# Three of eight granules of a down projection chunk by seven block products

## The chip, the cores and the metric

The kernel runs on one core of a Trainium2 chip. Its metric is the time of one execution on the device, in microseconds (us); smaller is better. The engines are named as the profile names them: PE (matmuls; PEld is its weight load), DVE, ACT, POOL, and SP, whose queue issues most transfers.

## The reference

One encoder layer for 256 tokens of 2048 channels in float32. A mixing sub-layer (gated short convolution and grouped attention side by side, gates, one merging projection) is followed by a squared-ReLU MLP:

```
h = rmsnorm(x, norm_mlp_pre[l])
f = jnp.square(jax.nn.relu(h @ w_up[l])) @ w_down[l]
x = x + rmsnorm(f, norm_mlp_post[l])
```

`w_up` is 2048 x 8192 and `w_down` 8192 x 2048. The change is in `f`, in the product with `w_down`.

## The kernel before

**Precision.** Each float32 operand is split into two float32r parts: hi is the value rounded (a copy on ACT), lo is the rest (a subtraction on DVE; `split`, lines 73 to 82). A product is then three matmuls: hi by hi, hi by lo, lo by hi.

**Granules and chunks.** Weights come in pieces of 128 x 512 per k-tile. A granule is two k-tiles: one transfer of 512 KB into a buffer `raw` (4 of them), one ACT copy into `whi`, one DVE subtraction into `wlo`, each 128 x 1024 (`weights`, line 137). A chunk is 512 output columns over 16 k-tiles, that is 8 granules. `granule` (line 121) hands out the `whi`/`wlo` buffers: from one ring of 4 in the mixing stage, and from two rings of 4 (`wts` and `wts2`, taken in turns of 4 granules) from the gates on.

**Two forms of a chunk.** `linear` (line 154) keeps tokens on the partitions of the result: for each granule 2 token halves x 2 k-tiles x 3 matmuls of 512 columns, lines 166 to 168. `linear_channels` (line 182) keeps channels there: 4 x 2 x 3 matmuls of 256 columns, lines 196 to 203. The last merging chunk, the first up chunk and the last down chunk use a `lag` of 4 granules: the second token half runs 4 granules behind the first.

**Order.** Code is written in program order, and a list scheduler sets each engine's order and the waits; on the chip DVE and ACT run theirs in that order. The MLP runs for q = 0 to 3: 4 up chunks (the first of all by `hidden`, the others by `hidden_channels`) that write the squared ReLU `f`, split, into the pair `A`, then 4 down chunks (`down`, line 666). At a down chunk's end `done` copies (q = 0, line 673) or adds (line 675) each token half into `facc`; for q = 3 it also takes squares on ACT and multiplies by a gain (line 680 or 683), and after the last chunk `finish` (line 655) scales and stores.

**Handover.** Between the merging projection and the MLP, `residual` (line 588) makes the MLP's normalised input `x2T` (pair `C`) for each token half: sum of squares, a power on POOL, 4 scaled additions (line 593), transposes on PE (line 598), a multiplication by a gain (line 601) and a split. The first up chunk's first token half needs that of t = 0, its second half that of t = 1.

Of the kernel before, what the change touches and what calls it, by code (L numbers as in the profile page):

```python
# [32 lines left out]
def trunk_kernel(  # L33
# [25 lines left out]
    WARM = 9  # L59

# [40 lines left out]
    step_in = [False]  # L101
# [19 lines left out]
    def granule():  # L121

        n = count[0]
        count[0] += 1
        pool = rings[n // WB % len(rings)]
        if pool is wts:
            return [pool.tile([P, KG, CH], F32R, name=name) for name in ("whi", "wlo")]
        if n % WB:
            return [pool.tile([P, KG, CH], F32R, name=name, bufs=WB - 1) for name in ("whi", "wlo")]
        out = []  # L130
        for name, spare, at in (("whi0", 32, (16, 32)), ("wlo0", 48, (48, 0))):
            flat = pool.tile([P, KG * CH + spare], F32R, tag=name, name=name[:3], bufs=1)
            at = at[step_in[0]]
            out.append(flat[:, at : at + KG * CH].rearrange("p (k c) -> p k c", k=KG))
        return out

    def weights(wv, k0, k1, ahead=None):

        for kd in range(k0, k1, KD):
# [6 lines left out]
            for kg in range(0, KD, KG):  # L146
                hi, lo = granule()
# [34 lines left out]
    def linear_channels(act, wv, done):  # L182
# [25 lines left out]
        end = []  # L208
        for gran in weights(wv, 0, KT):
# [6 lines left out]
        for c in range(0, CH // P, 2):  # L216
# [4 lines left out]
            tick(END // 2)  # L221

# [386 lines left out]
    rstd2_row = late.tile([P, T], F32, name="rstd2_row")  # L609
# [9 lines left out]
    facc = big.tile([P, 2, NT, D], F32, tag="B", name="facc")[:, 0]  # L619
# [3 lines left out]
    def hidden_channels(q, j, fT):  # L623


        def done(c, acc):
# [5 lines left out]
            split(f, fT[0][:, d : d + 2, :], fT[1][:, d : d + 2, :])  # L632

# [32 lines left out]
    def down(q, j, fT):  # L666
# [98 lines left out]
```

## Time and profile before

| what | value |
|---|---|
| median of 3 runs | 1597.08 us (1595.76 to 1598.09) |
| the profiled execution, its own time | 1597.23 us |
| its span, first to last instruction | 1595.5 us |
| PE busy | 1579.0 us (99%) |
| DVE busy | 947.7 us (59%) |
| ACT busy | 710.2 us (45%) |
| mean granted clock of PE | 0.998 of full speed |

Busy times are of the span. What PE shows as busy includes matmuls that overlap each other, so the pace of matmuls is read from their starts.

### The profile page before, as it was taken

What the parts mean: (1) busy time and instruction counts of PE and PEld (TensorE: products, weight loads), DVE (VectorE), ACT (ScalarE), POOL (GpSimd) and SP (SyncE); (2) the same over time, 40 slices, a digit from 0 to 9 for tenths busy, and PEclk for the clock granted to TensorE, in tenths of its full rate; (3) what the DMA queues carried; (4) which work ended last, traced back from release to release, by engine and by line L of the source; (5) the groups of instructions that cost most, each with busy time, mean ns of one, the idle gap of its engine ahead of it and who ended that gap; (6) DMA issues with size and microseconds to landing.
All of it is one profiled execution on the core that took longest, in us unless ns stands there. A gap on an engine that the chain in (4) does not pass through costs nothing.

```text
span 1595.5 us, 26862 instructions
## 1 busy us (share of the span) xinstructions
PE 1579.0 (99%) x11210; PEld 1468.5 (92%) x11210; DVE 947.7 (59%) x1107; ACT 710.2 (45%) x860; POOL 35.7 (2%) x23
## 2 busy tenths in 40 slices
PE   9999999999999999999999999999999999999997
PEld 7899999999999999999987799889988998899986
DVE  6767676677765554555554865446654565555654
ACT  7444444545454444444443644444433444334441
POOL 0110101001000000000000000000000000000000
PEclk9999999999999999999999999999999999999999
DMA  8655545555576565666763656656566665556662
GB/s 316 210 178 166 186 151 188 176 183 187 159 250 192 193 195 189 197 197 192 253 208 104 221 194 199 197 188 193 188 196 196 189 196 191 193 186 199 196 201 84
DMA packets 86297, 306.28 MB, mean 192 GB/s; under 512 B 9632, under 2 KB 10016, under 8 KB 85920
## 3 DMA queue, kind: packets, MB, share of 16 engines
q1 hardware_dynamic: 84608, 300.32, 58.1%
q10 hardware_dynamic: 1568, 4.25, 0.8%
q8 instruction: 87, 1.43, 0.4%
q14 instruction: 34, 0.28, 0.0%
HBM read 302.44 MB, written 2.10 MB: 191 GB/s over the span
## 4 chain that ended last, share of the span: by engine, by line
PE 97%; DVE 1%; DMA 1%; POOL 0%; ACT 0%; issue 0%; SPq 0%; DVEq 0%; POOLq 0%; ACTq 0%
PE acc L200 20%; PE acc L203 20%; PE acc L196 20%; PE acc L167 12%; PE acc L168 12%; PE acc L166 12%; DMA raw<-in_w_up 1%; PE at L402 0%; PE at L400 0%; PE at L401 0%; PE tr L433 0%; DMA raw<-in_w_in 0%; PE tr L245 0%; DVE wlo L77 0%; POOL rs L257 0%; ACT whi L76 0%
## 5 line engine op out<-in xcount | busy, mean ns | idle before, releaser
L77 DVE TENSOR_TENSOR wlo<-raw,whi 128x1024 fp32r<-128x1024 f32 (+1 forms) x561 | 684.4, 1222 | 563.1 <-ACT whi L76 562.3
L76 ACT CAST whi<-raw 128x1024 fp32r<-128x1024 f32 (+1 forms) x561 | 588.4, 1050 | 738.2 <-PE acc L200 366.8
L196 PE MATMUL acc<-A,whi 128*128 128x256 f32 x1280 | 355.9, 278 | 0.0
L203 PE MATMUL acc<-A,wlo 128*128 128x256 f32 x1280 | 353.8, 276 | 0.0
L200 PE MATMUL acc<-A,whi 128*128 128x256 f32 x1280 | 353.8, 276 | 0.0
L196 PE MATMUL acc<-C,whi 128*128 128x256 f32 x1216 | 336.8, 277 | 0.0
L203 PE MATMUL acc<-C,wlo 128*128 128x256 f32 x1216 | 336.6, 277 | 0.0
L200 PE MATMUL acc<-C,whi 128*128 128x256 f32 x1216 | 336.6, 277 | 0.0
L166 PE MATMUL acc<-whi,A 128*128 128x512 f32 x704 | 274.2, 391 | 2.2 <-ACT whi L76 2.2
L167 PE MATMUL acc<-wlo,A 128*128 128x512 f32 x704 | 275.2, 391 | 1.0 <-DVE wlo L77 1.0
L168 PE MATMUL acc<-whi,A 128*128 128x512 f32 x704 | 275.0, 391 | 0.0
L196 PEld LDWEIGHTS acc<-A,whi 128*128 128x128 f32 x1280 | 240.6, 188 | 0.2
L200 PEld LDWEIGHTS acc<-A,whi 128*128 128x128 f32 x1280 | 240.4, 188 | 0.2
L203 PEld LDWEIGHTS acc<-A,wlo 128*128 128x128 f32 x1280 | 240.3, 188 | 0.0
L196 PEld LDWEIGHTS acc<-C,whi 128*128 128x128 f32 x1216 | 228.7, 188 | 0.2
L200 PEld LDWEIGHTS acc<-C,whi 128*128 128x128 f32 x1216 | 228.7, 188 | 0.2
L203 PEld LDWEIGHTS acc<-C,wlo 128*128 128x128 f32 x1216 | 228.7, 188 | 0.0
L167 PEld LDWEIGHTS acc<-wlo,A 128*128 128x128 f32 x704 | 132.2, 188 | 30.9 <-DVE wlo L77 2.8
L166 PEld LDWEIGHTS acc<-whi,A 128*128 128x128 f32 x704 | 131.9, 188 | 30.8 <-ACT whi L76 3.1
L168 PEld LDWEIGHTS acc<-whi,A 128*128 128x128 f32 x704 | 132.2, 188 | 27.8
L196 PE MATMUL acc<-B,whi 128*128 128x256 f32 x256 | 70.7, 276 | 0.0
L200 PE MATMUL acc<-B,whi 128*128 128x256 f32 x256 | 70.7, 276 | 0.0
(144 smaller groups left out, 1115.6 us busy)
## 6 DMA issues: line engine op xcount, KB each, us to landing
raw<-in_w_in SPq DMA_DIRECT2D x207, 512.0 KB, 4.3
raw<-in_w_up SPq DMA_DIRECT2D x128, 512.0 KB, 3.5
raw<-in_w_dn SPq DMA_DIRECT2D x128, 512.0 KB, 3.3
raw<-in_w_oc SPq DMA_DIRECT2D x32, 512.0 KB, 4.5
raw<-in_w_oa SPq DMA_DIRECT2D x32, 512.0 KB, 4.2
raw<-in_w_mg SPq DMA_DIRECT2D x32, 512.0 KB, 4.4
xj<-in_x SPq DMA_DIRECT2D x4, 512.0 KB, 9.6
xr<-in_x ACTq DMA_DIRECT2D x1, 2048.0 KB, 9.7
```

The source lines that it names most:

```text
L76: nc.scalar.copy(hi, src)
L77: nc.vector.tensor_tensor(lo, src, hi.bitcast(F32), op=ALU.subtract)
L166: nc.tensor.matmul(accs[t], lhsT=ah[:, a, ts_], rhs=wh[:, g, :], start=first, stop=False)
L167: nc.tensor.matmul(accs[t], lhsT=ah[:, a, ts_], rhs=wl[:, g, :], start=False, stop=False)
L168: nc.tensor.matmul(accs[t], lhsT=al[:, a, ts_], rhs=wh[:, g, :], start=False, stop=last)
L196: nc.tensor.matmul(acc, lhsT=wh[:, g, cs], rhs=ah[:, a, :], start=a == 0 and c % 2 == 0, stop=False, skip_group_check=True,)
L200: nc.tensor.matmul(acc, lhsT=wh[:, g, cs], rhs=al[:, a, :], start=False, stop=False, skip_group_check=True)
L203: nc.tensor.matmul(acc, lhsT=wl[:, g, cs], rhs=ah[:, a, :], start=False, stop=a == KT - 1, skip_group_check=True)
```

## The change

In 15 of the 16 down chunks (not the last of q = 3) the granules of k-tiles 4, 8 and 12 are multiplied as 2 x 2 blocks: two token halves by two k-tiles, two k-tiles by two halves of 256 columns. In place of 8 block products of 256 columns (24 matmuls, issued as 12 of 512 columns) there are seven (21 matmuls of 256 columns), between sums of blocks:

- `seven` makes four sums of weight blocks on DVE (128 x 256 each) and splits 7 blocks in place of 4. Its buffers, `shi`, `slo` and `u`, are two each.
- `token_sums` makes four sums of token blocks of `f` in the up chunks (128 x 128 each) and splits them, 3 times for each q.
- `linear_sevens` adds the products into four banks of PSUM: the chunk's two accumulators and two more (`x1`, `x2`). `share` and the new lines of `done` add these into `facc` at the chunk's end.

The buffers change with it. The second ring `wts2` is closed before the MLP, whose granules then take one ring of 4, and whose up chunks take their first granule from `shi`/`slo`. The first up chunk so takes its first granules from `wts` and not from `wts2`. The pair `B` becomes two tiles.

```diff
+    def seven(raw):
+        hi, lo = [sevens[0].tile([P, 7, HC], F32R, name=name) for name in ("shi", "slo")]
+        u = sevens[0].tile([P, 4, HC], F32, name="u")
+        b = raw.rearrange("p k (n c) -> p (k n) c", n=2)
+        nc.vector.tensor_tensor(u[:, 0, :], b[:, 0, :], b[:, 1, :], op=ALU.add)
+        nc.vector.tensor_tensor(u[:, 2, :], b[:, 1, :], b[:, 3, :], op=ALU.add)
+        nc.vector.tensor_tensor(u[:, 1, :], u[:, 0, :], b[:, 3, :], op=ALU.add)
+        nc.vector.tensor_tensor(u[:, 3, :], u[:, 1, :], b[:, 2, :], op=ALU.add)
+        split(b[:, 0, :], hi[:, 0, :], lo[:, 0, :])
+        split(b[:, 2:4, :], hi[:, 1:3, :], lo[:, 1:3, :])
+        split(u, hi[:, 3:7, :], lo[:, 3:7, :])
+        return hi, lo
...
+            if a in BY_SEVEN:
+                w = [(hi[:, i, :], lo[:, i, :]) for i in range(7)]
+                r = [(x[0], x[1]) for x in (sums(BY_SEVEN.index(a), i) for i in range(4))]
+                last = a == BY_SEVEN[-1]
+                mm(x1[:, 0, :], tile_of(a, 0), w[0], 2, last)
+                mm(own[0], tile_of(a + 1, 0), w[1], 0, False)
+                mm(own[1], r[3], w[2], 0, False)
+                mm(x1[:, 1, :], r[0], w[3], 2, last)
+                mm(x2[:, 0, :], r[1], w[4], 3, last)
+                mm(x2[:, 1, :], r[2], w[5], 3, last)
+                mm(own[2], tile_of(a + 1, 1), w[6], 1, False)
...
+    merging.close()
+    rings.pop()
+    mlp = ctx.enter_context(tc.tile_pool(name="mlp", bufs=2))
...
+        r = wk.tile([P, 4, P], F32, tag="cc", bufs=CCB, name="cc")
+        nc.vector.tensor_tensor(r[:, 0, :], a21, a22, op=ALU.subtract)
+        nc.vector.tensor_tensor(r[:, 1, :], a11, r[:, 0, :], op=ALU.subtract)
+        nc.vector.tensor_tensor(r[:, 2, :], a21, a11, op=ALU.subtract)
+        nc.vector.tensor_tensor(r[:, 3, :], a12, r[:, 1, :], op=ALU.subtract)
+        split(r, rsum[:, n, 0], rsum[:, n, 1])
...
+            nc.scalar.copy(e[:, 0, :], x1[:, 0, :])
+            nc.vector.tensor_tensor(w[:, 0, :], x2[:, 0, :], e[:, 0, :], op=ALU.subtract)
+            nc.vector.tensor_tensor(e[:, 1, :], x1[:, 1, :], w[:, 0, :], op=ALU.add)
+            nc.vector.tensor_tensor(w[:, 0, :], x2[:, 1, :], w[:, 0, :], op=ALU.add)
+            nc.vector.tensor_tensor(w[:, 1, :], x1[:, 1, :], w[:, 0, :], op=ALU.add)
...
+                if t == 0:
+                    nc.vector.tensor_tensor(fj, fj, shared[0].rearrange("p n c -> p (n c)"), op=ALU.add)
+                else:
+                    nc.vector.tensor_tensor(f0, f0, shared[1][:, 0, :], op=ALU.subtract)
+                    nc.vector.tensor_tensor(f1, f1, shared[1][:, 1, :], op=ALU.add)
...
-    step_in[0] = True
-    rings.reverse()
+        if q == 3 and j == 3:
+            linear(fT, w_dn[j], done, q * KT, (q + 1) * KT, lag=LAG)
+        else:
+            linear_sevens(fT, sums, w_dn[j], done, q * KT)
```

Three places show how the order moves. Line numbers differ between the two kernels: 77 is 79 after the change, 582 is 660, 593 is 671, 601 is 679, 675 is 792, and 166 to 168 are 192 to 194.

First, DVE's order at the handover, from the residual of t = 0 to that of t = 1. Before (`acc_9348` is the last merging chunk's second token half, and `wlo_9597` to `wlo_9633` are the first four granules of the first up chunk):

```order
L593 SCALAR_TENSOR_TENSOR mg_9024<-mg_9024,rows1_8878,xr_8879 128x512
L77 TENSOR_TENSOR C_8881<-cc_9497,C_8881 128x4x128
L77 TENSOR_TENSOR wlo_9597<-raw_9594,whi_9596 128x1024
L601 TENSOR_TENSOR cc_9507<-at_9502,ch_104 128x512
L77 TENSOR_TENSOR wlo_9609<-raw_9606,whi_9608 128x1024
L77 TENSOR_TENSOR C_8881<-cc_9507,C_8881 128x4x128
L582 TENSOR_TENSOR mg_9024<-acc_9348,bias_9345 128x512
L560 TENSOR_REDUCE s1_9544<-ss01_101 128x1
L77 TENSOR_TENSOR wlo_9621<-raw_9618,whi_9620 128x1024
L256 TENSOR_SCALAR ms_9546<-s1_9544 128x1
L77 TENSOR_TENSOR wlo_9633<-raw_9630,whi_9632 128x1024
L593 SCALAR_TENSOR_TENSOR mg_9024<-mg_9024,rows1_8878,xr_8879 128x512 x3
```

After (the first up chunk's first four granules are `wlo_9605`, `wlo_9617`, `wlo_9629`, `wlo_9641`):

```order
L79 TENSOR_TENSOR wlo_9605<-raw_9602,whi_9604 128x1024
L79 TENSOR_TENSOR wlo_9617<-raw_9614,whi_9616 128x1024
L79 TENSOR_TENSOR wlo_9629<-raw_9626,whi_9628 128x1024
L660 TENSOR_TENSOR mg_9026<-acc_9349,bias_9347 128x512
...
L671 SCALAR_TENSOR_TENSOR mg_9026<-mg_9026,rows1_8880,xr_8881 128x512
L79 TENSOR_TENSOR wlo_9641<-raw_9638,whi_9640 128x1024
L679 TENSOR_TENSOR cc_9509<-at_9504,ch_104 128x512
L660 TENSOR_TENSOR mg_9026<-acc_9350,bias_9347 128x512
L638 TENSOR_REDUCE s1_9546<-ss01_101 128x1
L79 TENSOR_TENSOR C_8883<-cc_9509,C_8883 128x4x128
L333 TENSOR_SCALAR ms_9548<-s1_9546 128x1
L671 SCALAR_TENSOR_TENSOR mg_9026<-mg_9026,rows1_8880,xr_8881 128x512 x3
```

Three of the four weight splits have moved ahead of the whole chain of t = 0, and one is left ahead of t = 1.

Second, DVE's order in a down chunk of q = 1. Before, the end of one chunk with the splits on either side:

```order
L77 TENSOR_TENSOR wlo_12542<-raw_12539,whi_12541 128x1024
L77 TENSOR_TENSOR wlo_12560<-raw_12557,whi_12559 128x1024
L675 TENSOR_TENSOR facc_9590<-acc_12299,facc_9590 128x512
L675 TENSOR_TENSOR facc_9590<-acc_12300,facc_9590 128x512
L77 TENSOR_TENSOR wlo_12578<-raw_12575,whi_12577 128x1024
```

After, late in the second chunk (`raw_12933` and `raw_12987` are granules by seven of the third):

```order
L150 TENSOR_TENSOR u_12937<-raw_12933 128x256
L151 TENSOR_TENSOR u_12937<-raw_12933 128x256
L152 TENSOR_TENSOR u_12937<-u_12937,raw_12933 128x256
L79 TENSOR_TENSOR slo_12936<-raw_12933,shi_12935 128x256
L153 TENSOR_TENSOR u_12937<-u_12937,raw_12933 128x256
L79 TENSOR_TENSOR slo_12936<-raw_12933,shi_12935 128x512
L150 TENSOR_TENSOR u_12991<-raw_12987 128x256
L151 TENSOR_TENSOR u_12991<-raw_12987 128x256
L79 TENSOR_TENSOR slo_12936<-u_12937,shi_12935 128x1024
L79 TENSOR_TENSOR wlo_12972<-raw_12969,whi_12971 128x1024
L779 TENSOR_TENSOR cc_12876<-at_12682,cc_12875 128x256
L152 TENSOR_TENSOR u_12991<-u_12991,raw_12987 128x256
```

A granule by seven is seven DVE instructions in place of one, and the splits of the next chunk's first granules stand ahead of the row L779, which waits for the products in `x1` and `x2`.

Third, PE's order at the end of the last chunk, where t = 0 ends (`acc_15829` before, `acc_16911` after). Before:

```order
L167 MATMUL acc_15829<-wlo_15936,A_14344 128x512
L168 MATMUL acc_15829<-whi_15935,A_14344 128x512
L166 MATMUL acc_15830<-whi_15869,A_14344 128x512
L167 MATMUL acc_15830<-wlo_15870,A_14344 128x512
L168 MATMUL acc_15830<-whi_15869,A_14344 128x512
```

After:

```order
L193 MATMUL acc_16911<-wlo_17018,A_15207 128x512
L194 MATMUL acc_16911<-whi_17017,A_15207 128x512
L193 MATMUL acc_16912<-wlo_16964,A_15207 128x512
L194 MATMUL acc_16912<-whi_16963,A_15207 128x512
L192 MATMUL acc_16912<-whi_16981,A_15207 128x512
```

Before, 30 matmuls of t = 1 follow the last one of t = 0; after, 20 do.

## Rows read from the trace of the kernel before

**Rows 1.** The page: busy time, share of the span, instructions, by engine.

```profile
PE 1579.0 (99%) x11210; PEld 1468.5 (92%) x11210; DVE 947.7 (59%) x1107; ACT 710.2 (45%) x860; POOL 35.7 (2%) x23
```

**Rows 2.** The page: the chain that ended last, shares of the span by engine.

```profile
PE 97%; DVE 1%; DMA 1%; POOL 0%; ACT 0%; issue 0%; SPq 0%; DVEq 0%; POOLq 0%; ACTq 0%
```

**Rows 3.** Busy time by stage: mixing to merging, up chunks, down chunks of q = 1.

```profile
core 0: us, PE busy (x) PEld busy (x) DVE busy (x) ACT busy (x) POOL busy (x), PEclk, DMA share, GB/s
90.00:850.00 760.00, 760.00 (x6120) 737.22 (x6119) 465.19 (x563) 350.72 (x438) 16.92 (x6) 1.00 0.60 192
1062.00:1149.00 87.00, 87.00 (x765) 87.00 (x764) 50.23 (x51) 36.66 (x39) 0.00 (x0) 1.00 0.60 194
1150.00:1236.00 86.00, 86.00 (x380) 70.96 (x379) 44.95 (x43) 33.92 (x33) 0.00 (x0) 1.00 0.60 193
```

**Rows 4.** Timeline of PE (start, us): first matmuls of down, up, down stages.

```profile
974.40 0.39 PE L166 MATMUL acc<-whi,A 128*128 128x512 f32 x1
1061.77 0.28 PE L196 MATMUL acc<-C,whi 128*128 128x256 f32 x1
1149.44 0.39 PE L166 MATMUL acc<-whi,A 128*128 128x512 f32 x1
```

**Rows 5.** Groups by line and shape, whole run: busy us, mean ns | idle before.

```profile
L77 DVE TENSOR_TENSOR wlo<-raw,whi 128x1024 fp32r<-128x1024 f32 x559 | 683.0, 1224 | 562.0 <-ACT whi L76 561.3
L76 ACT CAST whi<-raw 128x1024 fp32r<-128x1024 f32 x559 | 587.2, 1052 | 737.4 <-PE acc L200 366.8 <-PE acc L168 247.5 <-issue 37.6
L675 DVE TENSOR_TENSOR facc<-acc,facc 128x512 f32<-128x512 f32 x24 | 15.5, 683 | 12.8 <-PE acc L168 12.8
L485 DVE TENSOR_TENSOR cv<-cv,bias 128x256 f32<-128x256 f32 x16 | 6.7, 418 | 0.0
```

**Rows 6.** Timeline of DVE where its queue is full: starts and durations, us.

```profile
226.99 0.42 DVE L485 TENSOR_TENSOR cv<-cv,bias 128x256 f32<-128x256 f32 x1
227.32 0.69 DVE L77 TENSOR_TENSOR pl<-tr,ph 128x512 fp32r<-128x512 f32 x1
227.92 0.42 DVE L485 TENSOR_TENSOR cv<-cv,bias 128x256 f32<-128x256 f32 x1
...
955.28 1.22 DVE L77 TENSOR_TENSOR wlo<-raw,whi 128x1024 fp32r<-128x1024 f32 x1
956.41 0.69 DVE L77 TENSOR_TENSOR A<-cc,A 128x512 fp32r<-128x512 f32 x1
```

**Rows 7.** Whom PE waited for: us in total, times, longest.

```profile
PE acc L166 <- ACT whi L76: 2.2, 2, 1.2
PE acc L167 <- DVE wlo L77: 2.2, 4, 0.8
PE acc L166 <- ACT C L76: 2.0, 1, 2.0
```

**Rows 8.** Timeline of PE at the handover, with the wait before.

```profile
875.76 0.39 PE L166 MATMUL acc<-whi,C 128*128 128x512 f32 x1
...
887.64 0.56 PE L166 MATMUL acc<-whi,C 128*128 128x512 f32 x1 [2.00 <-ACT C L76]
...
907.12 0.28 PE L196 MATMUL acc<-C,whi 128*128 128x256 f32 x1
```

**Rows 9.** Timeline of DVE, then of ACT, at the handover.

```profile
879.46 1.22 DVE L77 TENSOR_TENSOR wlo<-raw,whi 128x1024 fp32r<-128x1024 f32 x1
886.02 1.04 ACT L76 CAST whi<-raw 128x1024 fp32r<-128x1024 f32 x1 [1.65 <-DMA raw<-in_w_up]
886.97 1.65 ACT L76 CAST C<-cc 128x512 fp32r<-128x512 f32 x3
```

**Rows 10.** Timeline of DVE in the last 16 us.

```profile
1580.35 0.69 DVE L675 TENSOR_TENSOR facc<-acc,facc 128x512 f32<-128x512 f32 x1 [11.19 <-PE acc L168]
1584.77 0.75 DVE L663 SCALAR_TENSOR_TENSOR mg<-cc,rs,mg 128x512 f32<-128x512 f32 x1
1587.15 0.69 DVE L675 TENSOR_TENSOR facc<-acc,facc 128x512 f32<-128x512 f32 x1 [1.64 <-PE acc L168]
```

More of the change, by code (lines that the diff above doesn't have):

```diff
@@ L124, in granule, with weights @@
         count[0] += 1
-        pool = rings[n // WB % len(rings)]
[L126 to L137, printed above, removed]
+        if sevens and n % 8 == 0 and in_channels[0]:
+            return [
+                sevens[0].tile([P, 7, HC], F32R, name=name)
+                .rearrange("p b c -> p (b c)")[:, : KG * CH]
+                .rearrange("p (k c) -> p k c", k=KG)
+                for name in ("shi", "slo")
+            ]
+        pool = rings[n // WB % len(rings)]
+        return [pool.tile([P, KG, CH], F32R, name=name) for name in ("whi", "wlo")]
+    def seven(raw):
[10 more added lines that the diff above has]
+        return hi, lo
+    def weights(wv, k0, k1, ahead=None, by_seven=()):
         for kd in range(k0, k1, KD):
@@ L146, in weights @@
             for kg in range(0, KD, KG):
+                if kd - k0 in by_seven:
+                    count[0] += 1
+                    yield kd, *seven(raw)
+                    continue
                 hi, lo = granule()
@@ L221, in linear_channels, with linear_sevens, mm, tile_of @@
             tick(END // 2)
+        in_channels[0] = False
+    def linear_sevens(act, sums, wv, done, k0):
+        accs = [ps_acc.tile([P, CH], F32, name="acc") for _ in range(NT)]
+        own = [accs[0][:, :HC], accs[0][:, HC:], accs[1][:, :HC], accs[1][:, HC:]]
+        x1 = ps_tr.tile([P, 2, HC], F32, name="tr")
+        x2 = ps_at.tile([P, 2, HC], F32, name="at")
+        begun = set()
+        def mm(acc, a, w, bank, last):
+            nc.tensor.matmul(acc, lhsT=a[0], rhs=w[0], start=bank not in begun, stop=False, skip_group_check=True)
+            begun.add(bank)
+            nc.tensor.matmul(acc, lhsT=a[0], rhs=w[1], start=False, stop=False, skip_group_check=True)
+            nc.tensor.matmul(acc, lhsT=a[1], rhs=w[0], start=False, stop=last, skip_group_check=True)
+        tok = [slice(t * P, (t + 1) * P) for t in range(NT)]
+        def tile_of(a, t):
+            return act[0][:, a, tok[t]], act[1][:, a, tok[t]]
+        for k, hi, lo in weights(wv, k0, k0 + KT, by_seven=BY_SEVEN):
+            a = k - k0
+            if a in BY_SEVEN:
[10 more added lines that the diff above has]
+            else:
+                for t in range(NT):
+                    for g in range(KG):
+                        mm(accs[t], tile_of(a + g, t), (hi[:, g, :], lo[:, g, :]), t, a + g == KT - 1)
+                    if a + KG == KT:
+                        done(t, accs[t], x1, x2)
+            tick()
     def along_rows(dst, cols):
```

51 lines of the change are left out of this document (41 added, 10 removed).

## The prediction

> **What bounds the kernel now.** I read the page first, then the chain, the stages, and the starts of single instructions. PE is busy for 1579.0 of 1595.5 us [rows 1] and holds 97% of the chain that ended last [rows 2]. In the stages it is never idle: 760.00 of 760 us, 87.00 of 87, 86.00 of 86 [rows 3]. So time comes out of this kernel where PE gets less work, or at the few places where it waits, and other engines count only where they make PE wait. DVE works 44.95 of 86 us in a down stage and 50.23 of 87 in an up stage [rows 3]: about half is free. In all PE's waits for `whi`, `wlo` and the pair C come to 6.4 us [rows 7].
>
> A busy PE does not tell the price of a matmul, since they overlap. The starts do. Four down chunks run from 974.40 to 1061.77, that is 384 matmuls of 512 columns in 87.37 us, 0.2275 us each; four up chunks from there to 1149.44, 768 of 256 columns in 87.67 us, 0.1142 each [rows 4]. A matmul of 256 columns with a weight load of its own so costs half of one of 512.
>
> **PE's work.** A granule of 12 x 0.2275 = 2.730 us becomes 21 x 0.1142 = 2.397. That is 0.333 less, and 3 x 15 = 45 granules make it **-15.0 us**. The products by seven have the shape of an up chunk's matmuls (256 columns moved, weight of 128 x 128, three to a target), so I take that price as it stands. A chunk falls from 21.84 to 5 x 2.730 + 3 x 2.397 = 20.84 us.
>
> **DVE's work in a down chunk.** This decides. Lone durations are 1.224 us for 1024 columns, 0.683 for 512 and 0.418 for 256 [rows 5]. Where DVE's queue is full, the next instruction starts sooner: 0.33 after one of 256 (226.99 to 227.32), 0.60 after 512 (227.32 to 227.92), 1.13 after 1024 (955.28 to 956.41) [rows 6]. A granule by seven takes four sums and a split of 256 columns, a split of 512 and one of 1024:
>
> - at the starts of a full queue: 5 x 0.33 + 0.60 + 1.13 = 3.38;
> - at lone durations: 5 x 0.418 + 0.683 + 1.224 = 4.00.
>
> A chunk of q = 1 or 2 has five plain splits, three granules by seven, four steps of `share` that wait for each other (4 x 0.418 = 1.67 either way), and into `facc` three instructions of 512 and two of 256. The low end is 5.65 + 10.14 + 1.67 + 2.46 = 19.9 us, the high end 6.12 + 12.00 + 1.67 + 2.89 = 22.7, and PE's chunk lies between them at 20.84. I take about 20.5: the new instructions stand in one stretch, so the rows of a full queue are nearest, but some of the sums need the one before them. For q = 0 two instructions fall away (ACT copies instead), and for q = 3 two more of 512 come in (+1.2), for three chunks.
>
> [...]
>
> **What covers it.** DVE works ahead. A plain granule takes a buffer that was freed four plain ones before; a granule by seven one freed two by seven before. The tightest is the third: PE must be done with the first, and until it needs the third it has 2.73 + 2.40 + 2.73 = 7.86 us. The sums need no such buffer, so DVE owes the three splits in that time, about 2.1 us, behind ACT's copies of at most 1.05 [rows 5] at their end. Some 4.5 us are left. At a chunk's end DVE stands at the instruction that waits for the last products, with the next chunk's first granules split ahead of it. I find no place where PE must wait, with DVE at 98%, but bubbles will come: **+1.0 us**, between 0 and the 26 of the third rival below.
>
> ACT copies 7 blocks for 4: even at two copies of 1.05 for a granule by seven it has 5 x 1.05 + 3 x 2.1 = 11.6 us, and some 1 us at the end, of 20.84. The token sums add 4 x 0.418 + 0.68 = 2.4 us at most to three up chunks of each q, where DVE has 36.8 us of 87 free: nothing. Transfers are the same. One ring of 4 in the up chunks, in place of 8, costs nothing: the mixing stage ran on one ring of 4 with PE at 760.00 of 760 and DVE busier, 465.19 (61%) [rows 3].
>
> **The handover.** The first up chunk lasts from 875.76 to 907.12, 31.36 us [rows 8]. Its 96 matmuls at 0.2275 are 21.84, and 20 small ones (transposes and row sums) at no more than the 0.1142 of 256 columns are 2.3. The other 7.2 us are lost, 2.00 of them in the wait for the pair C that ends at 887.64 [rows 8]. Before, this chunk's first granules take buffers of `wts2`, which the last merging granules hold; so four splits of 1.2 us stand in DVE's queue around the chain of t = 1 (two of them, at 879.46 and after, inside it), and an ACT copy that waits for a transfer until 886.02 stands ahead of the copies of C at 886.97 [rows 9]. After, the buffers are those of the first merging granules: three splits are done before t = 0 begins, their transfers come early, and no weight copy stands between ACT's copies of C. Three splits at 1.13 are 3.4 us, and of the 1.65 that ACT waited for the transfer [rows 9] I add 0.6, since the two overlap in part: **-4.0 us**. Bounds: 0, if the row sums and the last four granules, which now wait for one ring of 4, give the gain back; -7.2, if all is recovered.
>
> **The tail.** t = 0 ends 20 matmuls before PE does, not 30: 4.55 us for 6.8. DVE's work for it lasts from 1580.35 to 1585.52, 5.17 us, and t = 1 starts with PE's end [rows 10]. It will now be 5.17 - 4.55 = **0.6 us** late.
>
> **Sum.** -15.0 - 4.0 + 1.0 + 0.6 = -17.4. The profiled execution took 1597.23 us, 1.73 more than its span and 0.15 above the median of 1597.08. From the median: **1579.7 us**.
>
> **The rivals.**
>
> *The handover gives nothing* (the row sums wait as long as before): 1583.7. For it: ACT's eight squares for the row sums stand ahead of the seventh granule's copy in its queue. Against: C's copies are free of weight copies.
>
> *DVE binds, with cover.* At lone durations a chunk of q = 1 or 2 is 22.67, 1.83 over PE's 20.84; 4 chunks make 7.3, less 4.5 of cover 2.8 us for each of the two. q = 0 (21.30) stays within its cover. q = 3 (24.04) is over by 3 x 3.2 = 9.6, less 4.5, 5.1. Together 10.7 in place of nothing: 1578.7 + 10.7 = 1589.4. For it: ACT and DVE hand each granule by seven to and fro, which leaves gaps. Against: the starts of a full queue.
>
> *DVE binds, without cover: slower.* At each chunk's end its queue stops at `share` until PE has done the third granule by seven, then until the chunk's end. If what it had ahead is used up there, every chunk pays its whole excess: 8 x 1.83 + 4 x 0.46 + 3 x 3.2 = 26.1, and 1578.7 + 26.1 = 1604.8. It decides from an excess of 18.4 / 15 = 1.2 us a chunk, a DVE chunk of 22.1 us with no lead. Against: the splits of the next chunk's first granules are queued ahead of that wait.
>
> *Products that cost more than half* would show in the up chunks, and don't.
>
> **How the numbers follow.** About 0.2% (3 us) is what a measurement here can tell from no change. My forecast has 0.68 (its own range 1576 to 1583), the handover without gain 0.08, DVE with cover 0.12, a result within 3 us of before (partial stalls) 0.04, slower 0.08. So faster 0.88, same 0.04, slower 0.08. The range holds the forecast, the first rival and most of the second: 1575.5 to 1589.5, with under 2 in 10 outside.
>
> **What would show it.** Steps: matmuls of 256 columns in the granules by seven start 0.114 apart; a down stage takes about 83.4 us instead of 87.4; DVE is busy for nearly all of it (by lone durations, more than its share) with starts near 0.33 apart after 256 columns; the first up chunk takes 27 to 28 us; the last additions of t = 1 start some 0.6 us after PE's end. I am wrong if PE's waits for `slo` or `shi` add up to more than some us, if a down stage takes 86 us or more, or if the first up chunk still takes 31.

## The result and the profile after

The changed kernel takes 1584.37 us (1583.51 to 1584.45, 3 runs) against 1597.08: a ratio of 0.9919 (95% interval [0.9897, 0.9942]; brackets behind a ratio are such an interval throughout), 12.7 us less. The forecast was 1579.7, so the gain is 4.7 us short of it. The profiled execution has a span of 1582.6 us, 12.9 less than before.

The page of the changed kernel (busy time by engine, then the chain by engine):

```profile
PE 1569.7 (99%) x11615; PEld 1477.9 (93%) x11615; DVE 1100.3 (70%) x1542; ACT 755.5 (48%) x977; POOL 34.7 (2%) x23
...
PE 92%; DVE 4%; DMA 2%; ACT 1%; issue 1%; POOL 0%; SPq 0%; DVEq 0%; POOLq 0%; ACTq 0%
```

Against [rows 1, 2], DVE has 153 us more and PE 9.3 less; 5% of the chain has left PE. Whom PE waited for, in us, times, longest:

```profile
PE acc L193 <- DVE wlo L79: 1.3, 3, 0.5
PE tr L271 <- DVE slo L79: 0.8, 1, 0.8
```

Beside [rows 7] this is little: these waits can't hold the missing 4.7 us. They are not all that PE loses: its weight loads (PEld) wait for `wlo` nine times, 4.2 us, where its matmuls show three waits. So what follows goes by starts. The lengths of stages can be had from PE's timeline, as from [rows 4, 8]. Before the change, beside those rows, the start of the down stage of q = 3 and the last matmul:

```profile
1499.52 0.39 PE L166 MATMUL acc<-whi,A 128*128 128x512 f32 x1
...
1586.73 0.39 PE L168 MATMUL acc<-whi,A 128*128 128x512 f32 x1
```

After the change (first up chunk, its successors, then down and up stages, the last chunk, the last matmul):

```profile
876.22 0.39 PE L192 MATMUL acc<-whi,C 128*128 128x512 f32 x1
...
902.44 0.28 PE L222 MATMUL acc<-C,shi 128*128 128x256 f32 x1
...
969.18 0.39 PE L269 MATMUL acc<-whi,A 128*128 128x512 f32 x1
...
1053.76 0.28 PE L222 MATMUL acc<-C,shi 128*128 128x256 f32 x1
...
1141.43 0.39 PE L269 MATMUL acc<-whi,A 128*128 128x512 f32 x1
...
1485.97 0.39 PE L269 MATMUL acc<-whi,A 128*128 128x512 f32 x1
...
1550.75 0.39 PE L192 MATMUL acc<-whi,A 128*128 128x512 f32 x1
...
1573.38 0.39 PE L194 MATMUL acc<-whi,A 128*128 128x512 f32 x1
```

Read the same way in all three kernels (the middle one is experiment 4 below, the changed kernel with its products by seven undone), us:

| stretch | before | products undone | after |
|---|---|---|---|
| start of the program to the first up chunk | 875.76 | 877.25 | 876.22 |
| first up stage | 98.64 | 92.96 | 92.96 |
| each other up stage | 87.67 | 87.67 | 87.67 to 87.70 |
| down stages of q = 0, 1, 2, each | 87.37 | 87.06 to 87.07 | 84.58 to 84.59 |
| down stage of q = 3, to its last matmul's start | 87.21 | 87.43 | 87.41 |
| from there to the end of the span | 8.72 | 9.18 | 9.21 |

Three stages give 2.79 us each where the forecast had 4.0, the fourth gives nothing, and the first up stage gives 5.7 where the handover had 4.0.

**A granule's pace.** The forecast priced a matmul of 256 columns at 0.1142 us, the mean of an up stage [rows 4]. That mean hides two paces. The kernel before, first three granules of an up chunk (the first starts at 1061.77 [rows 4]), each of 24 matmuls:

```profile
1064.64 0.28 PE L196 MATMUL acc<-C,whi 128*128 128x256 f32 x1
...
1067.36 0.28 PE L196 MATMUL acc<-C,whi 128*128 128x256 f32 x1
```

The first takes 2.87 us, the second 2.72: 0.120 and 0.1133 a matmul. After the change it is the same in an up chunk, and a granule by seven (21 matmuls from 1146.90) has a pace of its own:

```profile
1056.63 0.28 PE L222 MATMUL acc<-C,whi 128*128 128x256 f32 x1
...
1059.35 0.28 PE L222 MATMUL acc<-C,whi 128*128 128x256 f32 x1
...
1146.90 0.28 PE L269 MATMUL tr<-shi,A 128*128 128x256 f32 x1
...
1149.37 0.40 PE L269 MATMUL acc<-whi,A 128*128 128x512 f32 x1
```

2.47 us (2.476 in the mean of those that did not wait), 0.1179 a matmul, and 43 of all 45 take 2.47 or 2.48. The plain granule behind one takes 2.75 or 2.76, the others 2.72 (the first of a stage 2.74 or 2.75).

### The profile page after: what moved, and what is told of

Read it like the earlier page. It is cut to its first block, busy times and chain, and to the rows that moved or that the text cites. A ratio compares the mean times of both kernels' runs of the same rounds, so it can differ in the third digit from the quotient of the medians.

```text
span 1582.6 us, 28164 instructions
## 1 busy us (share of the span) xinstructions
PE 1569.7 (99%) x11615; PEld 1477.9 (93%) x11615; DVE 1100.3 (70%) x1542; ACT 755.5 (48%) x977; POOL 34.7 (2%) x23
## 4 chain that ended last, share of the span: by engine, by line
PE 92%; DVE 4%; DMA 2%; ACT 1%; issue 1%; POOL 0%; SPq 0%; DVEq 0%; POOLq 0%; ACTq 0%
PE acc L222 20%; PE acc L229 19%; PE acc L226 19%; PE acc L193 5%; PE acc L194 5%; PE acc L192 5%; PE acc L269 4%; PE acc L272 4%; PE acc L271 4%; DMA raw<-in_w_dn 2%; DVE wlo L79 1%; PE tr L269 1%; PE at L269 1%; PE tr L272 1%; PE at L272 1%; PE tr L271 1%
## 5 line engine op out<-in xcount | busy, mean ns | idle before, releaser
L79 DVE TENSOR_TENSOR wlo<-raw,whi 128x1024 fp32r<-128x1024 f32 (+1 forms) x501 | 609.7, 1221 | 381.7 <-ACT whi L78 380.6
L78 ACT CAST whi<-raw 128x1024 fp32r<-128x1024 f32 (+1 forms) x501 | 524.9, 1049 | 600.1 <-PE acc L226 331.8
L222 PE MATMUL acc<-C,whi 128*128 128x256 f32 x1096 | 302.7, 276 | 0.0
L229 PE MATMUL acc<-C,wlo 128*128 128x256 f32 x1096 | 302.5, 276 | 0.0
L226 PE MATMUL acc<-C,whi 128*128 128x256 f32 x1096 | 302.5, 276 | 0.0
L222 PEld LDWEIGHTS acc<-C,whi 128*128 128x128 f32 x1096 | 205.8, 188 | 0.0
L226 PEld LDWEIGHTS acc<-C,whi 128*128 128x128 f32 x1096 | 205.7, 188 | 0.0
L229 PEld LDWEIGHTS acc<-C,wlo 128*128 128x128 f32 x1096 | 205.7, 188 | 0.0
L269 PE MATMUL acc<-whi,A 128*128 128x512 f32 x300 | 117.9, 393 | 0.0
L272 PE MATMUL acc<-whi,A 128*128 128x512 f32 x300 | 117.1, 390 | 0.0
L271 PE MATMUL acc<-wlo,A 128*128 128x512 f32 x300 | 116.7, 389 | 0.0
L193 PE MATMUL acc<-wlo,A 128*128 128x512 f32 x224 | 88.8, 397 | 1.3 <-DVE wlo L79 1.3
L194 PE MATMUL acc<-whi,A 128*128 128x512 f32 x224 | 88.0, 393 | 0.0
L192 PE MATMUL acc<-whi,A 128*128 128x512 f32 x224 | 87.2, 395 | 0.4 <-ACT whi L78 0.4
L78 ACT CAST shi<-raw 128x512 fp32r<-128x512 f32 (+1 forms) x105 | 57.9, 588 | 54.0 <-DMA raw<-in_w_dn 31.1
L79 DVE TENSOR_TENSOR slo<-raw,shi 128x512 fp32r<-128x512 f32 (+1 forms) x105 | 66.5, 648 | 16.2 <-ACT shi L78 16.2
```

Source lines behind the costliest of these rows:

```text
L78: nc.scalar.copy(hi, src)
L79: nc.vector.tensor_tensor(lo, src, hi.bitcast(F32), op=ALU.subtract)
L192: nc.tensor.matmul(accs[t], lhsT=ah[:, a, ts_], rhs=wh[:, g, :], start=first, stop=False)
L193: nc.tensor.matmul(accs[t], lhsT=ah[:, a, ts_], rhs=wl[:, g, :], start=False, stop=False)
L194: nc.tensor.matmul(accs[t], lhsT=al[:, a, ts_], rhs=wh[:, g, :], start=False, stop=last)
L222: nc.tensor.matmul(acc, lhsT=wh[:, g, cs], rhs=ah[:, a, :], start=a == 0 and c % 2 == 0, stop=False, skip_group_check=True,)
```

## The experiments

Every kernel below computes the whole result. Executions of one kernel differ by some us (before: 1594.5 to 1599.2 over 25), much of it ahead of the stages that change (behind the same work, the first up chunk starts between 876.2 and 879.2 us), so lengths of stages are compared, and totals only beside them. The letters below are the expectations' own.

**1 to 3. Where the buffers start.** The first granule of an up chunk sits in `shi`/`slo` (S), which start at 64 modulo 256 bytes, as the activations C do; the others sit at 0, as the down stage's activations (A, `rsum`) do. Three kernels move S, and `u` behind it, by one number and nothing else:

```diff
-    rstd2_row = mlp.tile([P, T + 32], F32, name="rstd2_row", bufs=1)[:, :T]
+    rstd2_row = mlp.tile([P, T + 16], F32, name="rstd2_row", bufs=1)[:, :T]
```

(`T + 16` for S at 0, `T + 48` for 128, `T` for 192.)

> The pad of the tile ahead of the S tiles (shi, slo) goes from 32 to 16 columns, so that shi, slo and u start 64 bytes earlier and nothing else moves: counted modulo 256 bytes, S goes from 64 to 0, where the activations of the down stage (A, rsum) also start; the activations of the up stage (C) start at 64. Theory A: the pitch of 256-column matmuls hangs on how the start of the streamed operand stands to that of the loaded weights; in the changed kernel the only up granules at 0.120 us a matmul are those whose weights (S, 64) start where the streamed C does (64), the others (0 against 64) take 0.1133. By it the up granules in S fall from 2.88 to 2.72 us, and the granules by seven, now 0 against 0, rise from 2.48 to 2.52 us (21 x 0.120): 15 up chunks give back 2.4, 45 granules cost 1.8, about 1583.8 us in all. Theory B: the 2.48 us belong to the order of the products and their banks (seven blocks in four accumulators), whatever the address: granules by seven stay at 2.48, and only if the up granules move too does the time fall, to 1582.0. If neither moves, about 1584.4 and addresses are out.

> The same edit the other way: a pad of 48 columns, S at 128 modulo 256 bytes, equal to neither A and rsum (0) nor C (64). Theory A: both kinds of granule take 0.1133 us a matmul: up granules in S 2.72 us (15 x 0.16 = 2.4 us less), granules by seven 2.38 us (45 x 0.10 = 4.5 us less), about 1577.5 us. Theory B (products and banks): granules by seven stay at 2.48 us, at best 1582.0 for the up granules alone.

> No pad at all: S at 192 modulo 256 bytes. Theory A as told for 128: 2.72 and 2.38 us, about 1577.5 us, if only equal starts collide; if the distance matters too, the granules by seven differ between 64, 128 and 192, and the three runs together show how. Theory B: 2.48 us unchanged, about 1582.0 at best.

| S starts at | time, ratio to before | granule by seven | up granule in S | other up granules | an up stage | a down stage (q = 0 to 2) |
|---|---|---|---|---|---|---|
| 64 (after) | 1584.37, 0.9919 | 2.476 | 2.88 | 2.72 | 87.67 | 84.58 |
| 0 | 1596.38, 0.9999 [0.999, 1.0008] | 2.51 | 2.83 | 2.83 | 90.46 | 84.92 |
| 128 | 1586.86, 0.994 [0.9926, 0.9955] | 2.515 | 2.72, in 1 of 4 chunks 2.83 | the same | 87.90 | 85.15 |
| 192 | 1595.10, 0.9992 [0.9983, 1.0002] | 2.475 | 2.85 | 2.83 | 90.58 | 84.11 |

With S at 0 or 192 the times are those of the kernel before: the start of S alone takes the gain away (10.1 us of it, with S at 0, between the first up chunk and the last matmul). Theory B is out as I had put it, since the granules by seven go from 2.475 to 2.515 with S; that the order of the products and their banks has a part in the 0.1179 is not ruled out, because no place of S brings less. Theory A is out too: it had about 1577.5 us for S at 128 and 192, and by it the other up granules, none of whose operands moved, should have kept 2.72. They go with S. At 192 the granules by seven are no faster, but the plain granule behind one takes 2.72, and a down stage is 0.47 us shorter than with S at 64; the up stages take that back. With S at 128 one stage has both paces (PE's timeline; first three granules of the first chunk, then of the second):

```profile
1227.52 0.28 PE L222 MATMUL acc<-C,shi 128*128 128x256 f32 x1
...
1230.35 0.28 PE L222 MATMUL acc<-C,whi 128*128 128x256 f32 x1
...
1233.18 0.28 PE L222 MATMUL acc<-C,whi 128*128 128x256 f32 x1
...
1250.14 0.28 PE L222 MATMUL acc<-C,shi 128*128 128x256 f32 x1
...
1252.86 0.28 PE L222 MATMUL acc<-C,whi 128*128 128x256 f32 x1
...
1255.58 0.28 PE L222 MATMUL acc<-C,whi 128*128 128x256 f32 x1
```

2.83 and 2.83, then 2.72 and 2.72, with the same code and the same starts modulo 256. The windows of these two chunks (columns as in [rows 3]) show that neither the granted clock, 1.00 in both, nor idle time makes the difference:

```profile
1227.52:1250.14 22.62, 22.62 (x194) 22.62 (x192) 13.49 (x17) 8.57 (x9) 0.00 (x0) 1.00 0.64 208
1250.14:1271.90 21.76, 21.76 (x195) 21.76 (x193) 14.20 (x19) 9.30 (x11) 0.00 (x0) 1.00 0.61 192
```

In the up stages one pace thus lasts over whole chunks, and where S starts has a part in which one it is. With S at 0 the up stages stay at the slow one (first granule of a chunk, and the next):

```profile
1233.10 0.28 PE L222 MATMUL acc<-C,shi 128*128 128x256 f32 x1
...
1235.93 0.28 PE L222 MATMUL acc<-C,whi 128*128 128x256 f32 x1
...
1238.76 0.28 PE L222 MATMUL acc<-C,whi 128*128 128x256 f32 x1
```

The slow pace is 2.83 / 24 = 0.1179: that of the granules by seven.

**4. The products undone, the buffers kept.**

```diff
-            linear_sevens(fT, sums, w_dn[j], done, q * KT)
+            linear(fT, w_dn[j], done, q * KT, (q + 1) * KT, lag=LAG if q == 3 and j == 3 else 0)
...
-            token_sums(d, f)
```

> The arithmetic by seven is undone: all down chunks go through the plain product of eight blocks, the sums of tokens and of weights and the sharing at a chunk's end are gone; the one ring of four, the S tiles for one up granule in eight and the split tile B stay. The handover theory: the first up chunk keeps its 26.2 us against 31.4 before, whatever stands in the down stages, so this kernel is 5 to 6 us faster than the kernel before (about 1591.5 us). In the last chunk it also separates two causes of the 1.2 us that were lost there: if its waits come from the ring of four buffers (t=1 runs four granules behind), they stay here, some 0.6 us of 23.0 - 21.8; if they come from VectorE's additions for the shares, they are gone. Rival: the handover's gain came with the smaller queue of VectorE in the products by seven, then this kernel stands at 1597.

1594.27 us, 0.9986 [0.9977, 0.9996]. The total gained some 2 us, where 5 to 6 were expected, but the profiled execution, whose span is 4.4 us shorter than that of the kernel before, shows the handover's gain whole: from 877.25 to 903.47 the first up chunk takes 26.22 us, and the stage 92.96, both as after.

```profile
877.25 0.39 PE L192 MATMUL acc<-whi,C 128*128 128x512 f32 x1
...
903.47 0.28 PE L222 MATMUL acc<-C,shi 128*128 128x256 f32 x1
...
970.21 0.39 PE L192 MATMUL acc<-whi,A 128*128 128x512 f32 x1
```

So the handover's gain belongs to the buffers. Four more things do: each down stage of q = 0 to 2 loses 0.3 us (before, the first two granules of a chunk took 2.75 to 2.77); the last chunk gets 0.44 us longer from its first matmul to its last (22.13 us for 21.69; two of its runs of 12 matmuls take 2.97 and 2.99, where none took more than 2.78); the tail is 0.46 longer; and the merging stage takes 90.59 us for 89.24 (experiment 8). The first up chunk takes 5.14 of the stage's 5.67 us. The other 0.53 is pace: the last five granules of the second chunk are 0.1 us shorter each, most of them at 2.72 us where they took 2.83. What else the total lost, beside the span of the profiled execution, I can't place; executions of this kernel lie between 1592.2 and 1595.0 us. From this kernel to the changed one a down stage falls by 2.48: 12 granules by seven at 0.207.

**5. A start that might set the faster pace.** Three blocks of a granule by seven go to 0, four stay at 64:

```diff
-        hi, lo = [sevens[0].tile([P, 7, HC], F32R, name=name) for name in ("shi", "slo")]
+        both = [sevens[0].tile([P, 7 * HC + 64], F32R, name=name) for name in ("shi", "slo")]
+        hi, lo = [x[:, 16 : 3 * HC + 16].rearrange("p (b c) -> p b c", b=3) for x in both]
+        uh, ul = [x[:, 3 * HC + 32 : 7 * HC + 32].rearrange("p (b c) -> p b c", b=4) for x in both]
```

> Within a granule by seven, the first three weight blocks (nine matmuls) start at 0 modulo 256 bytes, as A and rsum do, and the four blocks of sums (twelve matmuls) at 64, where all seven start in the changed kernel; the up granules in S stay at 64. Theory A in its new form (the pace of 256-column matmuls is a state: one granule whose two operands start alike runs at 0.120 us a matmul, as the up granules in S do, and what follows it with unlike starts then runs at 0.1133 until something upsets it; without it, at 0.1177): the first nine take 0.120, the last twelve 0.1133, a granule 2.44 us and the kernel about 1.7 us less than 1584.4. Rival: equal starts cost 0.120 and unlike ones 0.1179 in a granule by seven whatever stands ahead; then 9 x 0.120 + 12 x 0.1179 = 2.495 us, and the kernel is 0.7 us slower. The pitch by place in the granule decides, over 45 granules.

1584.55 us, 0.9922 [0.9907, 0.9937]. A granule takes 2.49 us, as the rival said; nine matmuls, then twelve:

```profile
1147.76 0.28 PE L272 MATMUL tr<-shi,A 128*128 128x256 f32 x1
...
1148.84 0.28 PE L272 MATMUL tr<-shi,rsum 128*128 128x256 f32 x1
...
1150.25 0.40 PE L272 MATMUL acc<-whi,A 128*128 128x512 f32 x1
```

1.08 / 9 = 0.120 and 1.41 / 12 = 0.1175. Nine at equal starts do not bring the faster pace.

**6. Additions on GpSimd.**

```diff
-                    nc.vector.tensor_tensor(fj, fj, shared[0].rearrange("p n c -> p (n c)"), op=ALU.add)
+                    nc.gpsimd.tensor_tensor(fj, fj, shared[0].rearrange("p n c -> p (n c)"), op=ALU.add)
```

(and the two additions of `shared[1]`.)

> The three additions of shares to facc at each chunk's end (one of 512 columns, two of 256; 0.60 + 0.33 + 0.33 us of VectorE's queue) run on GpSimd instead. Theory V (the stalls of the last down stage come from VectorE's block of work at a chunk's end, which holds a raw buffer, so the transfer after it lands late, ScalarE's queue waits for it ahead of a cast of sums, and TensorE then waits for slo): 1.26 us a chunk less on VectorE takes away the stalls at the third granule by seven of the last stage (1.1 and 0.25 us) and most of the 0.6 us at the last chunk's start, 1582.5 to 1583 us. Rival: the stalls belong to the transfers themselves (landing 4.0 us against 3.3 before), whatever VectorE does: they stay, 1584.4. Second rival: GpSimd is several times slower at these additions and slows VectorE beside it, the stalls grow: above 1586.

1590.33 us, 0.9953 [0.9935, 0.9971]: the second rival, by total and by stages. The last down stage does lose the stalls that theory V spoke of (85.85 us to the last matmul's end, for 87.80), but those of q = 0 to 2 get some: 86.46, 84.89 and 87.61 for 84.58. That is 3.3 us more in all; another 2.9 of the profiled execution lie ahead of the first up chunk, where the work is the same. GpSimd's groups (busy us, mean ns | idle before), where DVE's means in the changed kernel are 685 and 419 ns:

```profile
L795 POOL TENSOR_TENSOR facc<-facc,cc 128x512 f32<-128x512 f32 x15 | 19.9, 1323 | 605.6 <-DVE facc L792 438.2 <-DVE cc L780 149.2 <-DVE cc L782 18.2
L799 POOL TENSOR_TENSOR facc<-facc,cc 128x256 f32<-128x256 f32 x15 | 19.5, 1303 | 0.0
```

And DVE's own work beside them gets longer: a subtraction of 128 x 512 takes 1.74 us here, for 0.69 in the mean of the changed kernel's 45 in granules by seven (0.77 in the mean of the 45 here). The first timeline is POOL's, the second DVE's, at the same place:

```profile
1389.17 1.30 POOL L795 TENSOR_TENSOR facc<-facc,cc 128x512 f32<-128x512 f32 x1 [18.53 <-DVE facc L792]
```

```profile
1389.27 1.74 DVE L79 TENSOR_TENSOR slo<-raw,shi 128x512 fp32r<-128x512 f32 x1
```

DVE's subtraction starts 0.10 us behind the start of GpSimd's addition and ends 0.54 us behind its end. What makes it longer was not shown.

**7. Six buffers in the last chunk.**

```diff
-        if sevens and n % 8 == 0 and in_channels[0]:
+        if sevens and (n % 8 == 0 and in_channels[0] or n % 4 == 0 and lagged[0]):
```

(`lagged[0]` is true in the last chunk alone.)

> In the last chunk, which is multiplied in eight blocks with its second half of tokens four granules behind, two of the eight granules go into the S tiles, so that six weight buffers are there instead of four. Theory R (in this chunk TensorE waits because casts wait for the ring of four, which the granules left behind hold): the three granules of 2.9 to 3.2 us that also stand in the kernel without products by seven go back to 2.72 to 2.76, 0.6 to 0.75 us less. Rival: casts come late there for VectorE's sake alone; then nothing changes within 0.2 us.

1582.32 us (1582.12 to 1582.79), 0.9907 [0.9893, 0.9922]. The last down stage takes 85.84 us, for 87.80, to its last matmul's end: 1.96 less, three times what theory R allows. Of three long runs of 12 matmuls in the last chunk (3.37, 2.92 and 2.94 us) one is left (2.90), and the chunk takes 22.01 us from its first matmul to its last, for 22.63: the size that theory R gave, but most of it is the 3.37, which experiment 4 with its ring of four does not have. The rest of the gain, 1.09 and 0.24 us, are stalls that stood in the third chunk and the second. In the changed kernel, third granule by seven of the third chunk (timeline of all engines):

```profile
1538.26 0.93 ACT L78 CAST shi<-raw 128x256 fp32r<-128x256 f32 x2
...
1543.29 1.05 ACT L78 CAST whi<-raw 128x1024 fp32r<-128x1024 f32 x1 [4.09 <-DMA raw<-in_w_dn]
...
1544.24 1.04 ACT L78 CAST shi<-u 128x1024 fp32r<-128x1024 f32 x1
...
1545.32 1.22 DVE L79 TENSOR_TENSOR slo<-u,shi 128x1024 fp32r<-128x1024 f32 x1 [1.22 <-ACT shi L78]
...
1546.60 0.39 PE L271 MATMUL tr<-slo,rsum 128*128 128x256 f32 x1 [0.84 <-DVE slo L79]
```

ACT waits 4.09 us for the transfer of the granule after next; the cast of the sums, which PE needs first, stands behind it. With six buffers the scheduler puts the sums first (ACT's timeline):

```profile
1537.08 0.93 ACT L78 CAST shi<-raw 128x256 fp32r<-128x256 f32 x2
1541.22 1.05 ACT L78 CAST shi<-u 128x1024 fp32r<-128x1024 f32 x1 [3.21 <-DVE u L154]
1544.23 1.05 ACT L78 CAST whi<-raw 128x1024 fp32r<-128x1024 f32 x1 [1.96 <-DMA raw<-in_w_dn]
```

The transfer is no earlier, 1544.23 for 1543.29, and PE doesn't wait: the granule takes 2.48 us, for 3.58. What made PE wait was the order on ACT together with a late transfer. The order by itself need not cost anything: in the second chunk it is the same in both kernels, and there the cast that waits starts 3.53 us ahead of the granule here and 2.00 in the changed kernel, whose granule took 2.72. Experiments 1, 2 and 5 keep the order in the third chunk too and have no stall, with that cast 2.3 to 2.7 us ahead, for 1.13. Why the transfer comes late in the changed kernel was not settled.

**8. The two halves of B change places.**

```diff
-            hi = big.tile([P, n + 3 * GAP], F32R, tag="B0", name="B")[:, at : at + n]
             lo = big.tile([P, n], F32R, tag="B1", name="B")
+            hi = big.tile([P, n + 3 * GAP], F32R, tag="B0", name="B")[:, at : at + n]
```

> Only the two halves of the split tile B change places, so that the low parts of the merge stage's activations start at 0 modulo 256 bytes (as in the kernel before) and not at 192; in the stages ahead of it the low parts of y then start at 0 where the high ones start at 192. In the changed kernel the merge stage's granules of twelve 512-column matmuls take 2.775 us, before 2.72: 1.35 us over the stage, which the prediction did not have. If the place of the low half makes this, the merge stage gives back about 1.4 us; the stage that reads y may lose as much or more, or nothing. If it doesn't, the merge stage stays at 90.6 us, and the new ring of weights beside it is the cause.

1588.32 us, 0.9942 [0.9927, 0.9958]. First and second granule of the merging stage, in the changed kernel and in this one:

```profile
785.39 0.39 PE L192 MATMUL acc<-whi,B 128*128 128x512 f32 x1
...
788.17 0.39 PE L192 MATMUL acc<-whi,B 128*128 128x512 f32 x1
```

```profile
790.30 0.39 PE L192 MATMUL acc<-whi,B 128*128 128x512 f32 x1
...
793.04 0.39 PE L192 MATMUL acc<-whi,B 128*128 128x512 f32 x1
```

2.78 and 2.74; the granules behind take 2.77 or 2.78 there and 2.72 here, as before. The stage that reads `y` loses more: the merging stage starts 4.9 us later, and 4.6 of them arise between 449 and 771 us. So the split of B costs the merging stage 1.35 us (90.59 for 89.24 between its first and last matmul, 89.03 here), and the place of the halves is why (experiment 12 moves the high one too).

**9. Other starts in the down stage.** A and `rsum` at 192, S at 0 for the products:

```diff
-    LATE = {"A": {"before": 0, "with": 16}
+    LATE = {"A": {"before": 0, "with": 0}
```

(with S's products at 0, S's up granules still at 64.)

> The activations of the down stage (A, rsum) start at 192 modulo 256 bytes in place of 0, and the products by seven read S at 0 (the up granules in S stay at 64): both kinds of down granule then read weights that start 64 bytes above their activations, where the changed kernel has 0 above for granules of eight and 64 above for those by seven. Theory A' (granules by seven are held at 0.1179 us a matmul by the granules of eight around them, which read equal starts): with unlike starts everywhere they fall to 0.1133, 2.38 us, some 4.4 us less: 1580.0. Theory A'' (the start alone sets a granule's pace, and 64 apart costs 0.1179 whatever stands around): 2.48 us stays, and with it about 1584.4. The granules of eight, at 2.72 us with equal starts, show whether 512 columns mind at all; 2.78 there, as in the merge stage, would cost 75 x 0.06 = 4.5 us.

1584.29 us, 0.9922 [0.9907, 0.9937]. Granules by seven take 2.475: theory A''. Plain ones all take 2.74 or 2.75 where they took 2.72 or 2.76. No start that I tried brings 0.1133 to the products. Over these runs starts of S and A that lie 64 bytes apart, either way, give 2.475 (S at 64 and 192, and this one), equal ones and ones 128 apart 2.51 to 2.515.

**10, 11. Four and two granules by seven.** `BY_SEVEN = (4, 6, 10, 12)` (with `rsum` at 192, for its size) and `(4, 12)`.

> Four of a chunk's eight granules by seven (4, 6, 10, 12) in place of three. TensorE's work falls by 15 x 0.23 = 3.5 us more; VectorE's rises by about 2.9 us a chunk (four sums, a cast more in three parts), from 18.9 to 20.5 us in the changed kernel's windows of 21.15 us to 22 and more, against a chunk of 20.9. Theory V (VectorE is the next limit, and the cover of raw and S buffers holds 4.5 us of lateness): chunks get as long as VectorE's work, 22 to 23.5 us, 15 to 35 us slower than 1584.4. Rival (VectorE's work is spread enough over the up stages, where it has room): stalls grow by a few us only, 1581 to 1585.

> Two granules by seven (4 and 12). If a granule by seven is worth 2.72 - 2.48 less about 0.01 for the granule behind it, 0.23 us, this kernel loses 15 x 0.23 = 3.5 us of the gain and, with less work on VectorE, gets back the stalls of the last down stage (1.4 us ahead of the last chunk and about 0.6 in it): 1586 to 1587. If products by seven were worth the 0.33 us that the prediction gave them, and stalls ate the rest evenly, taking one away would cost only what it frees, and this kernel would stand at or below 1584.4.

Four: 1588.03 us, 0.9949 [0.9932, 0.9965]. Down stages of q = 0 to 2 take 84.44 to 84.66, against 84.58 with three and 83.75 if the fourth were free of stalls: 0.7 to 0.9 us of stalls a stage. The last stage is 1.5 us longer. Both theories missed: VectorE begins to bind, by far less than its whole excess. Another 1.2 us lie in the first up stage, where most granules of its second and third chunk take 2.83 and not 2.72: the slower pace again, with the up operands at their old starts. Two: 1586.94 us, 0.9939 [0.9924, 0.9954], within the first theory's 1586 to 1587; a stage takes 85.41, so eight granules give (87.06 - 85.41) / 8 = 0.206 each, as twelve do.

**12. Six buffers, and both halves of the merging activations at 192.** Experiment 7 and

```diff
-    LATE = {"A": {"before": 0, "with": 16}, "B": {"before": 48, "with": 0}
+    LATE = {"A": {"before": 0, "with": 16}, "B": {"before": 48, "with": 48}
```

> Two edits: the two granules of the last chunk in the S tiles, which gave 1582.3 us, and the high parts of the merge stage's activations at 192 modulo 256 bytes, where the split tile left the low ones (in the changed kernel 0 and 192; before, both at 0). If the merge stage's 2.775 us a granule come from the two halves' unlike starts, it falls to 2.72 or, as in the down stage with activations at 192, 2.745 us: 0.9 to 1.7 us less, 1580.7 to 1581.4 us in all, and the stage that reads y, whose operands stay, keeps its time. If any half at 192 costs this, the merge stage keeps 90.6 us or gets longer, and the kernel stays at 1582.3 or above.

1583.01 us (1581.92 to 1584.31), 0.9916 [0.9902, 0.9929]. Merging granules take 2.745, the stage 89.81 us for 90.59, the last down stage 85.84. So the stage gave back 0.8 us, a little under the least that was expected, and the total missed its 1580.7 to 1581.4: the profiled span, 1580.1, is 2.5 less than the changed kernel's, but the times can't tell this kernel from experiment 7.

## Why the prediction was right, and where its sum was off

By stage, forecast and measured, us:

| term | forecast | measured | how |
|---|---|---|---|
| PE's work | -15.0 | -9.30 | 45 x 0.207 (experiments 4 and 11) |
| handover | -4.0 | -5.14 | first up chunk, 31.36 to 26.22 |
| second up chunk | 0 | -0.53 | its last granules at 2.72 for 2.83 |
| new buffers in down stages | 0 | -1.24 | 4 x 0.31 (experiment 4; for q = 3 taken as in the others) |
| stalls | +1.0 | +2.37 | the last stage: +0.20 where -1.86 and -0.31 were due |
| tail | +0.6 | +0.49 | 8.72 to 9.21 |
| ahead of the first up chunk | 0 | +0.46 | merging +1.35, the rest -0.9, which varies between executions |

These make -12.9, the difference of the spans. The mechanism was right: less work on PE and a shorter handover, with DVE's work covered in three stages of four. The sum was not. The result lies outside the forecast's own range (1576 to 1583) and inside the wide one, close to the time of the first rival (1583.7), whose cause, a handover without gain, is out. That is luck in part: the 5.7 us that PE's work fell short and 1.4 of stalls were partly made up by 1.1 of handover and 1.8 that no term held. Of the signs of being wrong one came, a down stage of 86 us or more: that of q = 3.

**PE's work: the term that was mis-sized.** "I take that price as it stands" failed. The last rival, products that cost more than half, was dismissed because it "would show in the up chunks, and don't"; it did show there, in one granule of eight (0.120 us a matmul, where half of a plain one is 2.72 / 24 = 0.1133), and I had read a mean. Of the 0.126 us that a granule by seven gives less than forecast, 0.079 is its own pace (2.476 for 2.397), 0.037 the plain granule behind it (2.75 to 2.76 for 2.72), and 0.010 that a plain granule was 2.72 and not 2.730. That pace hangs on the operands' starts is shown (1 to 3); why a granule by seven has 0.1179, and whether anything gives it 0.1133, stays open: four places of S, one other of A and a mixed one did not, and the order of the products and their banks was never changed.

**DVE's work** came out at what was taken or a little under. Its starts in a full queue stand 0.33 to 0.34 apart after 256 columns (1495.71, 1496.05, 1496.38), not at the 0.42 of a lone one. Three chunks of q = 1, windows of the changed kernel (columns as in [rows 3]):

```profile
1141.43:1162.58 21.15, 21.15 (x125) 18.70 (x124) 18.98 (x35) 12.99 (x19) 0.00 (x0) 1.00 0.63 199
1162.58:1183.70 21.12, 21.12 (x124) 18.69 (x123) 19.55 (x35) 10.55 (x15) 0.00 (x0) 1.00 0.63 198
1183.70:1204.85 21.15, 21.15 (x124) 18.69 (x123) 20.45 (x37) 10.21 (x14) 0.00 (x0) 1.00 0.61 187
```

19 to 20.5 us of 21.15, and PE idle nowhere; all twelve chunks of q = 0 to 2 take 21.13 to 21.17. So the cover that the forecast described holds there, and both rivals in which DVE binds are out for these stages. For q = 3 they are not ruled out (below). Lone durations were no price from start to start: by them the forecast had 22.7 us for the 35 instructions of a chunk, and the first two of these windows have 35 each, in 21.15 and 21.12.

**Stalls** came where the excess was forecast largest, q = 3, but by two ways that the forecast did not name: a late transfer that ACT's order puts ahead of the urgent cast (experiment 7), worth 1.1 us in the third chunk, and 0.24 us of lateness at the same place of the second; and 0.94 us in the last chunk. Of these 0.44 stand in experiment 4 too, where the lag of 4 granules meets one ring of 4. The rest is one run of 12 matmuls that takes 3.37 us, and 2.72 in experiments 4, 6 and 11, all with less work on DVE (and in 10, with more, where PE came to it later). In experiments 6 and 11 the stalls of the second and third chunk are gone as well. So DVE's work may have a part in q = 3, as the rivals had it, but this is not shown: experiments 1, 2 and 5 lose the stalls of the second and third chunk with DVE's work unchanged. "One ring of 4 in the up chunks ... costs nothing" was right of the up chunks; it left out the last down chunk. The first wait of that chunk, for a DVE subtraction behind the sharing, is in PE's timeline:

```profile
1555.57 0.50 PE L193 MATMUL acc<-wlo,A 128*128 128x512 f32 x1 [0.35 <-DVE wlo L79]
```

**Handover.** The first up chunk takes 26.2 us, for 31.4 and a forecast of 27 to 28; the 2.00 us wait of [rows 8] is gone. Its bounds held, and experiment 4 shows that it owes nothing to the products. It was undersized by 1.1 us; which of the lost 7.2 us came back beyond the splits and the transfer stays open.

**Tail.** The first addition for t = 1 starts 0.58 us behind the end of PE's last matmul (1573.38 + 0.39):

```profile
1574.35 0.69 DVE L792 TENSOR_TENSOR facc<-acc,facc 128x512 f32<-128x512 f32 x1
```

It stands behind DVE's work for t = 0, which began at 1569.28, 5.07 us earlier. In experiment 7 t = 0 ends earlier on PE: its addition starts 5.97 us ahead of that for t = 1 (1566.22 and 1572.19), which starts with PE's end, and the tail is back at 8.67 us. So the term was right in size and cause.

## What to carry to other kernels

Price new matmuls by the single granule and as a range, not by the mean of a stage: two granules of one shape here differ by 6% (0.1133 and 0.120 us a matmul), and the 0.1179 of the new ones lies between. When a change moves buffers, look again at every stage whose operands moved, and at chunks with a lag; one number in a pad was worth the whole change here (1596.38 us for 1584.37, experiment 1). And where two casts stand in one queue, the one whose consumer comes first should stand first: the late transfer of experiment 7 cost nothing once nothing urgent was queued behind it.

## What the runs showed of the hardware

Float32r matmuls of 256 columns showed at least three paces at a granted clock of 1.00: 0.1133, 0.1179 and 0.120 us. Which one holds hung on where the buffers start (given here modulo 256 bytes; other steps than 64 bytes were not tried): with S at 0 in place of 64, and nothing else moved but `u` behind it, most up granules went from 2.72 to 2.83 us and those by seven from 2.476 to 2.51 (experiment 1). In the up stages it hung on something else too: granules with the same starts take 2.72 or 2.83 us within one execution, chunk by chunk, at the same granted clock (experiment 2). At 512 columns the same shows smaller: 2.72, 2.745 or 2.775 us for twelve (experiments 8, 9, 12). The mechanism behind it was not found.
